# Weight halves for the output projection prepared by GpSimd one stage sooner, a third output tile begun early, and loads of the seam put behind dense products

## The chip, the cores and the metric

One core of one Trainium2 chip. The metric is the device time of one execution in microseconds; a smaller time is better. The engines are named as in the profile: PE is TensorE (matrix products; PEld its weight loads), DVE is VectorE, ACT is ScalarE, POOL is GpSimd, SP is SyncE, which here does nothing but issue DMA transfers.

## What is computed

One layer of a hybrid model over 2048 latent tokens and 128 context tokens, 1024 channels, all in float32. Cut to what matters:

```python
h = rmsnorm(x) * (1 + scale) + shift
proj = h @ w_in                                    # 1024 -> 4096
r, k, v, g_a, b_gate, c_gate, u_conv, g_b = split(proj)
r, k, v = token_shift(r, k, v)
# 8 heads of 64 channels, run forwards and backwards over the tokens:
#   S = S * w_t - (S kk_t) (kk_t a_t)^T + v_t k_t^T ;  y_t = S r_t
ya, s_final = wkv(h, r, k, v, s0)                  # group norm and bonus inside
ya = ya * silu(g_a)
yb = b_gate * short_conv(c_gate * u_conv) * silu(g_b)
u  = concat([ya, yb]) @ w_out                      # 1024 -> 1024
out = rmsnorm(x + gate * u)                        # and s_final of the context
```

The first 512 rows of `w_out` meet the recurrent half `ya` (called ATT in the kernel, k = 0 to 3 in blocks of 128), the last 512 the convolution half `yb` (CONV, k = 4 to 7). `yb` needs nothing of the recurrence.

## The kernel before, in words

Phase 1 is the input projection and the convolution half, in thirds of the tokens. Each of its products is kept near float32 by splitting both operands into a high part in the reduced format fp32r and the remainder: hi x hi, hi x lo, lo x hi, three matmuls for one. `yb` and, later, `ya` go to a scratch tensor `mixT` in memory.

Phase 2 is the recurrence in chunks of 64 tokens. It has 17 stages (`NST`), each of two groups of 8 chunk-and-head units, one for each direction; one of them is for the context. A stage is made of generators: `partL` loads its operands, `partI` solves its triangular systems (`solve_steps`, on POOL for most stages, `by_vector` on DVE for two), `partW` makes `psF`, `psG` and their results, `partB` makes `psX` and `psE`, `partU` makes `psU` and `psW` from `zc` (the loaded result of the solve, transposed to `zr`), and `partS` runs the state recurrence `psS` with `sv` and ends with `psT` and the group norm on `y`. The letters of the strings `ROUND` and, for the last two stages, `ROUND_END` give the order in which the generators of stage s (S, own B) and of stage s + 1 (L, u/U, B) are advanced. So while the states of stage s run, stage s + 1 is prepared. `early()` runs the first stage's parts inside the last dense products of phase 1; this place is called the seam (about 900 to 1005 us).

Phase 3 is the output projection: 17 tiles of 128 tokens, each of two halves of 512 columns, each half of 8 k-blocks of three matmuls of 128x512. `load_raw` loads a block of `w_out` (tile `woraw`), `load_k` makes its high part `woh` and its remainder `wol`; `load_m` does the same with 128 tokens of `mixT` (`mxc`, `mhc`, `mlc` for the convolution half, `mxa`, `mha`, `mla` for the recurrent one). The raw tiles `woraw`, `mxc` and `mxa` share two buffers of one tag, so a load waits until both readers of the tile before the last are done. Two output tiles, 5 and 6, have their convolution half done ahead, in the last stages of phase 2: the generator `ahead()` is advanced after each S of the ring. It first makes the four convolution weights, then for each tile the 12 products of each half into `psa`, stored in `z0`. `tail()` goes on with the recurrent weights and the full tiles (`psu`).

The written order is only the start. The queue of each engine is set by a scheduler that runs a simulated timeline over all the code, so an instruction may stand far ahead of its place in the text when its inputs and its tile are there. `behind(instruction, after)` adds an order between two instructions without a wait for data. On one engine the queue is then strictly in order; SP's queue holds nearly all loads and stores. `spare` puts a tile into the place of an operand that is no longer used.

## Time and profile before

| what | value |
|---|---|
| time, three runs | 1651.35, 1651.52, 1659.19 us, median 1651.52 |
| the profiled execution | 1657.8 us, span 1656.0 us |
| mean granted clock of TensorE | 0.969 |
| busy | PE 1538.7 us, DVE 1108.4, ACT 766.8, POOL 569.0 |
| transfers | 327.23 MB, mean 198 GB/s |
| phase 1 | to about 1005 us |
| the last POOL solve | stored at 1317.04 us |
| first product of phase 3 | 1466.21 us |

Times inside the profile count from the start of the span. The profiled execution lies 6.3 us above the median of the runs, as one of the three runs does. A busy row of the page divides the span into 40 slices of 41.4 us, a digit for each, in tenths.

### The profile page before, as it was taken

The numbers are of one execution on the slowest core, as the hardware profiler recorded it, in microseconds if no ns is written. First come the engines' busy times: TensorE is split into PE (matmuls) and PEld (weight loads), VectorE is DVE, ScalarE is ACT, GpSimd is POOL, SyncE is SP. The second block draws the span as 40 slices with busy tenths as digits, with TensorE's granted clock in tenths as the row PEclk, the third lists the DMA queues.
The fourth block names the chain that finished last, engine by engine and source line by source line (L and its number), as shares of the span: only waits on it lengthen the run. The fifth ranks groups of instructions, "written<-read, shape, count | busy, mean of one in ns | idle before, by whom it ended". The sixth has DMA issues, their size and how long they took to land.

```text
span 1656.0 us, 42386 instructions
## 1 busy us (share of the span) xinstructions
PE 1538.7 (93%) x17160; PEld 1412.4 (85%) x17160; DVE 1108.4 (67%) x2226; ACT 766.8 (46%) x1623; POOL 569.0 (34%) x1028
## 2 busy tenths in 40 slices
PE   5899999999999999999999899988988888789998
PEld 2899998999999999999988898878887777668886
DVE  5876977784738775658787883576775765574333
ACT  4544565553425353435554013667675665432222
POOL 0011211110102121112765564888888700022221
PEclk8899999999999999999999999999999989889999
DMA  9677767664746465655858768676767643264342
GB/s 377 205 263 249 244 234 276 218 225 178 241 140 208 166 207 183 200 202 186 271 165 270 237 201 239 179 192 180 204 175 195 169 131 102 66 198 160 127 149 93
DMA packets 237988, 327.23 MB, mean 198 GB/s; under 512 B 91288, under 2 KB 191896, under 8 KB 223712
## 3 DMA queue, kind: packets, MB, share of 16 engines
q1 hardware_dynamic: 231840, 318.55, 60.8%
q0 software_dynamic: 1200, 3.93, 0.6%
q8 instruction: 135, 2.21, 0.6%
q10 hardware_dynamic: 4752, 2.04, 0.5%
q14 instruction: 61, 0.50, 0.1%
HBM read 207.92 MB, written 116.54 MB: 196 GB/s over the span
## 4 chain that ended last, share of the span: by engine, by line
PE 47%; DVE 10%; ACT 7%; DMA 4%; issue 3%; POOL 3%; SPq 0%; DVEq 0%; ACTq 0%; POOLq 0%
PE psu L1380 4%; PE psu L1381 4%; PE psu L1382 4%; PE psE L840 3%; PE psS L840 2%; ACT fg L829 2%; PE psX L840 2%; PE psW L840 1%; PE mmg L166 1%; PE mmg L168 1%; PE mmg L167 1%; PE mmc L166 1%; PE mmc L167 1%; PE mmu L167 1%; PE mmu L166 1%
## 5 line engine op out<-in xcount | busy, mean ns | idle before, releaser
L950 POOL TENSOR_TENSOR zt<-zt,ztmp 128x30 f32<-128x30 f32 (+7 forms) x390 | 153.3, 393 | 30.6
L840 PE MATMUL psE<-fg 128*64 128x128 f32 x2176 | 135.8, 278 | 17.4 <-ACT fg L831 15.2
L840 PEld LDWEIGHTS psE<-fg 128*64 128x64 f32 x2176 | 120.8, 139 | 24.1 <-ACT fg L831 17.8
L840 PE MATMUL psS<-sv,E 128*64 128x64 f32 x2176 | 99.5, 235 | 19.3 <-DVE sv L1147 18.4
L840 PEld LDWEIGHTS psS<-sv,E 128*64 128x64 f32 x2176 | 82.5, 144 | 35.5 <-DVE sv L1147 24.4
L329 POOL TENSOR_TENSOR shk<-rawl 128x384 f32<-128x384 f32 (+1 forms) x24 | 24.8, 1033 | 242.9 <-ACT rawl L325 223.8
L829 ACT ACTIVATE fg<-psX 64x512 f32<-64x512 f32 x136 | 80.4, 591 | 44.9 <-PE psX L840 42.8
L1147 DVE TENSOR_TENSOR sv<-psS,pc 64x128 f32<-64x128 f32 x254 | 63.9, 277 | 43.6 <-PE psS L840 41.4
L947 POOL TENSOR_TENSOR ztmp<-ab,zt 128x60 f32<-128x60 f32 (+4 forms) x165 | 85.1, 516 | 12.9
L1447 POOL TENSOR_TENSOR z<-z,x 128x512 f32<-128x512 f32 x32 | 41.7, 1304 | 138.3 <-DVE z L1443 114.8
L329 POOL TENSOR_TENSOR shv<-rawl 128x384 f32<-128x384 f32 (+1 forms) x24 | 20.8, 866 | 164.5 <-ACT rawl L325 164.4
L1041 DVE TENSOR_TENSOR F<-psF,consts 128x512 f32<-128x512 f32 x68 | 44.0, 681 | 46.5 <-PE psF L840 46.5
L831 ACT COPY fg<-psG 64x256 f32<-64x256 f32 x136 | 49.8, 366 | 52.4 <-DVE fg L1048 46.3
L1048 DVE TENSOR_TENSOR fg<-psG,consts 64x256 f32<-64x256 f32 x136 | 57.3, 421 | 24.0 <-ACT fg L831 11.7
L166 PE MATMUL mmc<-h,w 128*128 128x384 f32 (+1 forms) x192 | 64.8, 337 | 5.9 <-ACT q1r L327 4.1
L446 POOL COPY pcs<-pp 128x6 f32<-128x6 f32 (+1 forms) x48 | 21.0, 437 | 139.2 <-ACT pp L435 138.9
L166 PE MATMUL mmg<-h,w 128*128 128x384 f32 (+1 forms) x192 | 64.3, 335 | 3.8 <-ACT q1v L327 3.8
L831 ACT COPY E<-psE 128x256 f32<-128x256 f32 x136 | 48.4, 373 | 37.8 <-DVE E L1109 27.9
L1109 DVE TENSOR_TENSOR E<-psE,consts 128x256 f32<-128x256 f32 x136 | 53.0, 418 | 19.0 <-PE psE L840 17.6
L166 PE MATMUL mmb<-h,w 128*128 128x384 f32 (+1 forms) x192 | 62.9, 328 | 1.5 <-ACT ta L439 1.5
L166 PE MATMUL mmgb<-h,w 128*128 128x384 f32 (+1 forms) x192 | 64.0, 333 | 0.3 <-ACT q1r L327 0.3
L168 PE MATMUL mmg<-h,w 128*128 128x384 f32 (+1 forms) x192 | 64.0, 334 | 0.0
(323 smaller groups left out, 5173.3 us busy)
## 6 DMA issues: line engine op xcount, KB each, us to landing
w<-scr_wsp SPq DMA_DIRECT2D x68, 1024.0 KB, 5.7
scr_wsp<-w SPq DMA_DIRECT2D x34, 1024.0 KB, 4.9
scr_ops<-pair SPq DMA_DIRECT2D x80, 384.0 KB, 4.0
wr<-in_win SPq DMA_DIRECT2D x34, 512.0 KB, 5.9
o<-scr_ops SPq DMA_DIRECT2D x32, 512.0 KB, 6.6
fg<-scr_ops SPq DMA_DIRECT2D x120, 128.0 KB, 3.5
x<-in_x SPq DMA_DIRECT2D x17, 512.0 KB, 8.5
wadas<-in_wada SPq DMA_DIRECT2D x8, 1024.0 KB, 13.5
```

The costliest lines, as they stand in the source:

```text
L166: T.matmul(ps[:, :n], w[:, 0, k], hh[:, 0, k, :n], start=k == 0, stop=False)
L168: K.dense = T.matmul(ps[:, :n], w[:, 1, k], hh[:, 0, k, :n], start=False, stop=k == 7).ins
L829: P.activation(dst, src, AF.Copy, scale=-1.0)
L831: P.copy(dst, src)
L840: r = T.matmul(*a, start=True, stop=True, **k)
L947: eng.tensor_tensor(tv, ab[:, j:j + 2, j + 2:32].unsqueeze(1).broadcast_to((128, kn, 2, n)), zt[:, :kn, j:j + 2].unsqueeze(3).broadcast_to ...
L950: last = eng.tensor_tensor(zt[:, :kn, j + 2:32], zt[:, :kn, j + 2:32], tv[:, :, r], ALU.subtract).ins
L1048: V.tensor_tensor(g.gs[H[1 - h], g.op, h, us], ps[gi][r, :, 64:128], B.mG[r, g.d].unsqueeze(1).broadcast_to((64, 4, 64)), ALU.mult)
L1147: r = V.tensor_tensor(dst, sp[gi][0:64, q], B.pc[0:64, d, 2 * p:2 * p + 2, c:c + 1].broadcast_to((64, 2, 64)), ALU.mult)
L1380: T.matmul(ps[:], mh[:, n], hi[:, cs], start=start and n == 0, stop=False)
L1381: T.matmul(ps[:], mh[:, n], lo[:, cs], start=False, stop=False)
L1382: T.matmul(ps[:], ml[:, n], hi[:, cs], start=False, stop=stop and n == 3)
```

## The change

It has two places. In the late stages: the four convolution weights and their halves are made by POOL (`G`) in place of ACT (`P`) and DVE (`V`); so are the halves of the tokens that go with them. `weights()` and `ahead()` start one stage sooner (s == NST - 4), and only the PSUM pool stays where it was (`open_sums`). The order of the weights is 6, 7, 4, 5, since 4 and 5 lie in places of operands that are in use longer. A third tile, 7, is done ahead, and `products` is called for one k-block, three matmuls, at a time. At the seam: the stores of the two solves on DVE are kept and issued behind dense products that come later, the loads of stage 1 are put behind such products too (`B.mid`), and `center_states` is cut in two.

```diff
+        store = lambda by: by(S["zt"][s].rearrange("h u s b q i -> (h u s b) (q i)"), zf)
+        if eng is G:
+            store(G.dma_start)
+        else:
+            B.kept.append([3, store])
...
-                load_half(g, half(g, n), D)
+                load_half(g, half(g, n), D if s != 1 else lambda *a: behind(D(*a), B.mid[1 if n else g.d]))
...
+    def put_back():
+        for x in B.kept:
+            x[0] -= 1
+        while B.kept and B.kept[0][0] <= 0:
+            behind(B.kept.pop(0)[1](D), K.dense)
+            B.mid.append(K.dense)
...
+            if s == NST - 4:
+                K.weights()
+                tail = K.ahead()
             if s == NST - 3:
                 O.pm.close()
                 O.pm = None
-                K.weights()
-                tail = K.ahead()
+                K.open_sums()
...
-    AHEAD = TILES[:2]
+    PREP = (6, 7, 4, 5)
+    AHEAD = TILES[:3]
...
+        copy = P.copy if raw is None else G.tensor_copy
         raw = raw or load_raw(k)
-        P.copy(hi[:], raw[:])
+        copy(hi[:], raw[:])
...
-        P.copy(mh[:], mx[:])
-        V.tensor_tensor(ml[:], mx[:], mh[:].bitcast(F32), ALU.subtract)
+        copy(mh[:], mx[:])
+        eng.tensor_tensor(ml[:], mx[:], mh[:].bitcast(F32), ALU.subtract)
...
-        for n, k in enumerate(CONV):
-            load_k(k, *[...], V, O.raw[n])
+        for n, k in enumerate(PREP):
+            load_k(k, *[...], G, O.raw[n])
             if n < 2:
-                O.raw.append(load_raw(CONV[n + 2]))
-            yield
+                O.raw.append(load_raw(PREP[n + 2]))
+            if n != 1:
+                yield
+            else:
+                for _ in range(5):
+                    yield
         for i in AHEAD:
-            ms = load_m(O.r, i, CONV, 1)
+            ms = load_m(O.r, i, CONV, 1, G.tensor_copy, G)
...
-                products(ps, ms, HALF[h], CONV, True, True)
+                for n in range(4):
+                    products(ps, ms, HALF[h], CONV, True, True, n)
+                    if n < 3:
+                        yield
                 P.copy(z0[i][:, HALF[h]], ps[:])
                 yield
```

What the scheduler makes of it shows in the queues. First POOL, from the store of the last solve (`scr_zt`) to the recurrent weights; `sv` is the tile of the states that is set to zero for a stage, `held` its value kept for the next. Before:

```order
L955 DMA scr_zt_66<-zt_1124_15938 128x512
L970 MEMSET sv_1207_17780 64x128 x4
L970 MEMSET sv_1208_17786 64x128 x4
L1129 COPY sv_1231_18310<-held_1219_18159 64x128
L1129 COPY sv_1232_18312<-held_1220_18166 64x128
L1361 TENSOR_TENSOR wol1_18861<-woraw1_18862,woh1_18860 128x1024
L1361 TENSOR_TENSOR wol0_18855<-woraw0_18856,woh0_18854 128x1024
L1361 TENSOR_TENSOR wol2_18867<-woraw2_18868,woh2_18866 128x1024
L1361 TENSOR_TENSOR wol3_18873<-woraw3_18874,woh3_18872 128x1024
```

After:

```order
L955 DMA scr_zt_66<-zt_1124_15938 128x512
L1385 CAST woh4_17675<-woraw4_17448 128x1024
L1386 TENSOR_TENSOR wol4_17676<-woraw4_17448,woh4_17675 128x1024
L1397 CAST mhc5_17913<-mxc5_17911 128x512
L1398 TENSOR_TENSOR mlc5_17914<-mxc5_17911,mhc5_17913 128x512
L974 MEMSET sv_1207_17796 64x128 x4
L974 MEMSET sv_1208_17802 64x128 x4
L1385 CAST woh5_17871<-woraw5_17486 128x1024
L1386 TENSOR_TENSOR wol5_17872<-woraw5_17486,woh5_17871 128x1024
L1397 CAST mhc6_18394<-mxc6_18392 128x512
L1398 TENSOR_TENSOR mlc6_18395<-mxc6_18392,mhc6_18394 128x512
L1397 CAST mhc7_18813<-mxc7_18811 128x512
```

`woh4` to `mlc6` stand behind the last solve, the casts and subtracts of tile 5 ahead of the two memsets, those of `woh5` and tile 6 behind them; tile 7's and the four recurrent `wol` follow.

The other two weights, 6 and 7, stand much earlier on POOL, inside a solve (`ztmp` and `zt` are its tiles; the row numbers are from 357 on of 791):

```order
L947 TENSOR_TENSOR ztmp_911_11021<-ab_909_11015,zt_910_11020 128x220
L950 TENSOR_TENSOR zt_910_11020<-zt_910_11020,ztmp_911_11021 128x5x22
L1385 CAST woh6_17444<-woraw6_17300 128x1024
L950 TENSOR_TENSOR zt_910_11020<-zt_910_11020,ztmp_911_11021 128x5x22
L1385 CAST woh7_17482<-woraw7_17302 128x1024
L1386 TENSOR_TENSOR wol6_17445<-woraw6_17300,woh6_17444 128x1024
L947 TENSOR_TENSOR ztmp_911_11021<-ab_909_11015,zt_910_11020 128x240
L1386 TENSOR_TENSOR wol7_17483<-woraw7_17302,woh7_17482 128x1024
L950 TENSOR_TENSOR zt_910_11020<-zt_910_11020,ztmp_911_11021 128x6x20 x2
L947 TENSOR_TENSOR ztmp_911_11021<-ab_909_11015,zt_910_11020 128x252
```

Before, the same place holds the solve's rows alone.

SP at that time, early in phase 2 (`woraw` are the raw weights, `zc` the solve's result for stage 2, `ab` the next solve's input). Before:

```order
L1185 DMA sg_965_12528<-scr_sg_61 128x512
L1354 DMA woraw4_17735<-in_wout 128x1024
L1354 DMA woraw5_17737<-in_wout 128x1024
L998 DMA fg0_9816<-scr_ops0_57 64x2x256 x2
L998 DMA fg1_9817<-scr_ops1_58 64x2x256 x2
L889 DMA a1_10972<-scr_lo_65 128x256 x2
L1027 DMA zc_933_11608<-scr_zt_66 64x16x32 x2
L925 DMA ab2_913_11102<-scr_at_64 32x1024 x4
L987 DMA sv_931_11604<-scr_vt_60 64x1024
L987 DMA sv_932_11606<-scr_vt_60 64x1024
```

After:

```order
L1190 DMA sg_965_12528<-scr_sg_61 128x512
L1378 DMA woraw6_17300<-in_wout 128x1024
L1378 DMA woraw7_17302<-in_wout 128x1024
L1003 DMA fg0_9816<-scr_ops0_57 64x2x256 x2
L1003 DMA fg1_9817<-scr_ops1_58 64x2x256 x2
L889 DMA a1_10972<-scr_lo_65 128x256 x2
L1378 DMA woraw4_17448<-in_wout 128x1024
L1378 DMA woraw5_17486<-in_wout 128x1024
L1032 DMA zc_933_11608<-scr_zt_66 64x16x32 x2
L992 DMA sv_931_11604<-scr_vt_60 64x1024
L992 DMA sv_932_11606<-scr_vt_60 64x1024
```

All four raw weights now go out here; 4 and 5 take the buffers of 6 and 7, whose readers are on POOL.

SP in the late stages, with the token blocks `mxc` and the operands of the stage that comes next. Before:

```order
L1354 DMA woraw6_17895<-in_wout 128x1024
L1001 DMA fg0_9816<-scr_ops0_57 64x2x128 x4
L1001 DMA fg1_9817<-scr_ops1_58 64x2x128 x4
L1354 DMA woraw7_17933<-in_wout 128x1024
L1369 DMA mxc5_18058<-scr_mixT_63 128x4x128
L1001 DMA fg0_9816<-scr_ops0_57 64x2x128 x4
L1001 DMA fg1_9817<-scr_ops1_58 64x2x128 x4
L1369 DMA mxc6_18169<-scr_mixT_63 128x4x128
L1185 DMA sg_1203_17739<-scr_sg_61 128x512
L1027 DMA zc_1209_17792<-scr_zt_66 64x16x32
L1221 DMA scr_mixT_63<-yo_1198_17535 128x512
L1027 DMA zc_1209_17792<-scr_zt_66 64x16x32
```

After:

```order
L1006 DMA fg0_9816<-scr_ops0_57 64x2x128 x4
L1006 DMA fg1_9817<-scr_ops1_58 64x2x128 x4
L1394 DMA mxc5_17911<-scr_mixT_63 128x4x128
L1394 DMA mxc6_18392<-scr_mixT_63 128x4x128
L1006 DMA fg0_9816<-scr_ops0_57 64x2x128 x4
L1006 DMA fg1_9817<-scr_ops1_58 64x2x128 x4
L1190 DMA sg_1203_17755<-scr_sg_61 128x512
L1032 DMA zc_1209_17808<-scr_zt_66 64x16x32
L1226 DMA scr_mixT_63<-yo_1198_17554 128x512
L1032 DMA zc_1209_17808<-scr_zt_66 64x16x32
```

The two raw weights are gone from here, and tile 6's `mxc6` stands ahead of the second four-piece loads `fg`.

PE, where the products of tile 7 (`psa7`) are put, between the group norm's `psT` and `psW`, `psF` and `psX` of stage 15. Before:

```order
L840 MATMUL psS14_0_4_17986<-sv_1187_17334,E_1213_17857 64x64 x4
L840 MATMUL psS14_1_4_17992<-sv_1188_17336,E_1214_17869 64x64 x4
L847 MATMUL psT1215_18002<-consts_9809,y_1091_15179 128x2x64 x4
L840 MATMUL psW15_18011<-zc_1209_17792,zr_1212_17855 32x32 x32
L840 MATMUL psS14_0_4_17986<-sv_1187_17334,E_1213_17857 64x64 x4
L840 MATMUL psS14_1_4_17992<-sv_1188_17336,E_1214_17869 64x64 x4
L840 MATMUL psF15_0_1_18087<-fg0_9816,o30_10973 64x128 x2
L840 MATMUL psF15_1_1_18088<-fg1_9817,o31_10974 64x128 x2
```

After:

```order
L840 MATMUL psS14_0_4_18007<-sv_1187_17341,E_1213_17877 64x64 x4
L840 MATMUL psS14_1_4_18013<-sv_1188_17343,E_1214_17889 64x64 x4
L847 MATMUL psT1215_18023<-consts_9809,y_1091_15179 128x2x64 x4
L1407 MATMUL psa7_0_18818<-woh4_17675,mhc7_18813 128x512
L1408 MATMUL psa7_0_18818<-wol4_17676,mhc7_18813 128x512
L1407 MATMUL psa7_1_18832<-woh4_17675,mhc7_18813 128x512
L1408 MATMUL psa7_1_18832<-wol4_17676,mhc7_18813 128x512
L840 MATMUL psW15_18032<-zc_1209_17808,zr_1212_17875 32x32 x32
L840 MATMUL psS14_0_4_18007<-sv_1187_17341,E_1213_17877 64x64 x4
L840 MATMUL psS14_1_4_18013<-sv_1188_17343,E_1214_17889 64x64 x4
L840 MATMUL psF15_0_1_18091<-fg0_9816,o30_10973 64x128 x2
```

Four of tile 7's 24 products stand here; sixteen more follow behind the first `psX15`, four in `psG15`. Up to this place PE's order is the same in both kernels but for the places of `psa5` and `psa6`.

More of the change, by code (lines that the diff above doesn't have):

```diff
@@ L954, in solve_steps @@
             O.solved = last
-        (G.dma_start if eng is G else D)(S["zt"][s].rearrange("h u s b q i -> (h u s b) (q i)"), zf)
+        store = lambda by: by(S["zt"][s].rearrange("h u s b q i -> (h u s b) (q i)"), zf)
[3 more added lines that the diff above has]
+            B.kept.append([3, store])
     def by_vector(s, d):
@@ L1226, in phase2 @@
     K.mixed = {}
+    def put_back():
[4 more added lines that the diff above has]
+            B.mid.append(K.dense)
     def early():
         setup_first()
-        center_states()
+        B.kept, B.mid = [], []
+        center = center_states()
+        next(center)
         partI(2)
@@ L1236, in early @@
         sts[0] = partL(0, K.dense)
+        for _ in center:
+            pass
         next(vec)
@@ L1243, in early @@
             next(vec, None)
+            put_back()
             yield
@@ L1248, in early @@
             next(vec, None)
+            put_back()
             yield
@@ L1251, in early @@
             pass
+        while B.kept:
+            put_back()
         B.bb = bb
@@ L1357, in load_k, with load_m @@
     def load_k(k, hi, lo, eng, raw=None):
+        copy = P.copy if raw is None else G.tensor_copy
         raw = raw or load_raw(k)
-        P.copy(hi[:], raw[:])
+        copy(hi[:], raw[:])
         eng.tensor_tensor(lo[:], raw[:], hi[:].bitcast(F32), ALU.subtract)
         wk[k] = (hi, lo)
-    def load_m(pool, i, ks, b):
+    def load_m(pool, i, ks, b, copy=P.copy, eng=V):
         t0 = i * 128
@@ L1371, in load_m, with products @@
         ml = pool.tile([128, 4, 128], F32R, tag=f"ml{a}", name=f"ml{a}{i}", bufs=b)
-        P.copy(mh[:], mx[:])
-        V.tensor_tensor(ml[:], mx[:], mh[:].bitcast(F32), ALU.subtract)
+        copy(mh[:], mx[:])
+        eng.tensor_tensor(ml[:], mx[:], mh[:].bitcast(F32), ALU.subtract)
         return mh, ml
-    def products(ps, ms, cs, ks, start, stop):
+    def products(ps, ms, cs, ks, start, stop, only=None):
         mh, ml = ms
         for n, k in enumerate(ks):
+            if only not in (None, n):
+                continue
             hi, lo = wk[k]
@@ L1387, in weights, with open_sums @@
         O.r = Pool(K, "p3r", "left")
+        O.raw = [load_raw(k) for k in PREP[:2]]
+    def open_sums():
         O.pr = Pool(K, "p3pr", "right", 2, PSUM)
         O.pu = O.pr
-        O.raw = [load_raw(k) for k in CONV[:2]]
     def ahead():
         yield
-        for n, k in enumerate(CONV):
-            load_k(k, *[K.spare(f"wo{a}{k}", F32R, f"o{k - 3}{m}") if n < 2 else O.r.tile([128, 1024], F32R, name=f"wo{a}{k}") for m, a in enumerate("hl")], V, O.raw[n])
+        for n, k in enumerate(PREP):
+            load_k(k, *[K.spare(f"wo{a}{k}", F32R, f"o{k - 3}{m}") if k < 6 else O.r.tile([128, 1024], F32R, name=f"wo{a}{k}") for m, a in enumerate("hl")], G, O.raw[n])
             if n < 2:
-                O.raw.append(load_raw(CONV[n + 2]))
-            yield
+                O.raw.append(load_raw(PREP[n + 2]))
[4 more added lines that the diff above has]
+                    yield
         for i in AHEAD:
-            ms = load_m(O.r, i, CONV, 1)
+            ms = load_m(O.r, i, CONV, 1, G.tensor_copy, G)
             if i not in z0:
-                z0[i] = K.spare(f"z0_{i}", F32, "ab2" if z0 else "ab")
+                z0[i] = K.spare(f"z0_{i}", F32, ("ab", "ab2")[len(z0)]) if len(z0) < 2 else O.r.tile([128, 1024], F32, name=f"z0_{i}")
             for h in range(2):
                 ps = O.pr.tile([128, 512], F32, tag="u", name=f"psa{i}_{h}")
-                products(ps, ms, HALF[h], CONV, True, True)
+                for n in range(4):
+                    products(ps, ms, HALF[h], CONV, True, True, n)
+                    if n < 3:
+                        yield
                 P.copy(z0[i][:, HALF[h]], ps[:])
@@ L1463, in rest @@
             p.close()
-    K.weights, K.ahead, K.tail, K.rest = weights, ahead, tail, rest
+    K.weights, K.open_sums, K.ahead, K.tail, K.rest = weights, open_sums, ahead, tail, rest
 def layout3(I):
```

## The prediction

> **What bounds the kernel now.** I read the page first, then the late part in windows cut at the first matmul of each stage's `psU`, then what TensorE waits for in each window, then the groups of the operations that change hands.

> ```profile
> PE 1538.7 (93%) x17160; PEld 1412.4 (85%) x17160; DVE 1108.4 (67%) x2226; ACT 766.8 (46%) x1623; POOL 569.0 (34%) x1028
> PE   5899999999999999999999899988988888789998
> PE 47%; DVE 10%; ACT 7%; DMA 4%; issue 3%; POOL 3%; SPq 0%; DVEq 0%; ACTq 0%; POOLq 0%
> ```

> TensorE is busy 93% of the span and holds 47% of the chain that ended last, so time is won only where its row shows less than 9, or by taking matmuls off it. The change takes none off it. Its row has one long weak stretch, the 8s and the 7 from the 27th digit on (each digit is 41.4 us). The windows show that stretch stage by stage; I call them window 13 (from psU13 to psU14, the third row), 14, 15 and 16, and the last row is the start of phase 3.

> ```profile
> core 0: us, PE busy (x) PEld busy (x) DVE busy (x) ACT busy (x) POOL busy (x), PEclk, DMA share, GB/s
> 1194.10:1218.70 24.60, 21.96 (x586) 19.56 (x586) 18.49 (x45) 15.04 (x32) 21.23 (x48) 1.00 0.72 193
> 1298.90:1322.10 23.20, 21.47 (x588) 19.42 (x588) 18.40 (x45) 15.00 (x32) 15.95 (x34) 1.00 0.69 187
> 1322.10:1353.90 31.80, 25.20 (x582) 21.77 (x583) 20.10 (x47) 20.65 (x40) 0.00 (x0) 0.89 0.47 126
> 1353.90:1394.30 40.40, 38.05 (x632) 31.64 (x630) 18.05 (x45) 21.11 (x42) 1.26 (x8) 0.87 0.37 102
> 1394.30:1423.20 28.90, 23.91 (x570) 20.74 (x570) 18.77 (x45) 15.62 (x33) 2.91 (x3) 0.94 0.32 84
> 1423.20:1466.20 43.00, 28.72 (x604) 24.39 (x604) 27.44 (x69) 19.14 (x37) 7.43 (x3) 0.86 0.45 142
> 1466.20:1512.00 45.80, 45.79 (x192) 37.06 (x193) 27.03 (x41) 13.47 (x33) 11.95 (x9) 0.95 0.54 173
> ```

> An undisturbed stage lasts 23.2 to 24.6 us. Window 13 has the same count of matmuls (582) and lasts 31.8: ACT is up from 15.0 to 20.65 us, DVE from 18.4 to 20.1, POOL does nothing. Window 14 holds 48 more products. Phase 3 runs TensorE without a gap, 192 products in 45.79 us, 0.2385 us each. What TensorE waits for, window by window (13; 14; 15; 16 with the first product of phase 3):

> ```profile
> PE psS L840 <- DVE sv L1147: 2.6, 2, 1.6
> PE psF L840 <- ACT E L831: 2.0, 1, 2.0
> PE psE L840 <- ACT fg L831: 1.1, 1, 1.1
> PE psG L840 <- ACT fg L829: 0.5, 1, 0.5
> ...
> PE psE L840 <- ACT fg L831: 2.0, 1, 2.0
> ...
> PE psE L840 <- ACT fg L831: 3.3, 1, 3.3
> PE psF L840 <- ACT fg L829: 1.1, 1, 1.1
> ...
> PE psT L847 <- DVE y L1202: 4.4, 1, 4.4
> PE psu L1380 <- ACT mha L1372: 4.1, 1, 4.1
> ```

> **The change, part by part.** First what it takes from ACT and DVE in windows 13 and 14. The rows are the cast of a weight block on ACT, its subtract on DVE, the same subtract where GpSimd does it already, and the largest one-input operation that GpSimd has (a memset of half that width):

> ```profile
> L1360 ACT CAST woh<-woraw x4: 1034/1044/1044, 1333.1 to 1367.2; 128x1024 fp32r<-128x1024 f32 x4
> L1361 DVE TENSOR_TENSOR wol<-woraw,woh x4: 1173/1225/1226, 1334.2 to 1368.3; 128x1024 fp32r<-128x1024 f32 x4
> L1361 POOL TENSOR_TENSOR wol<-woraw,woh x4: 2336/2346/2778, 1406.5 to 1456.5; 128x1024 fp32r<-128x1024 f32 x4
> L935 POOL MEMSET zt<- x13: 524/529/533, 900.7 to 1289.0; 128x512 f32 x13
> 1317.04 0.61 POOL L955 DMA_DIRECT2D scr_zt<-zt  x1 [0.30 <-POOL zt L950]
> 1364.13 0.63 POOL L970 MEMSET sv<- 64x128 f32 x4 [46.48 <-PE psS L840]
> ```

> Three of the four casts and subtracts (1333 to 1348 us) fall into window 13: 3 x 1.04 = 3.1 us of ACT and 3 x 1.22 = 3.7 us of DVE, between a chain PE to ACT to DVE to PE that waits for these two engines by turns (6.2 us of waits in the rows above). With them on GpSimd, which ends its last solve at 1317.04 and then idles 46.48 us, window 13 has the work of the row 1194.1 or 1298.9. I take 24.5, the worse of them: **-7.3 us** (-8.6 at 23.2; 0 if the stall only moves). Nobody waits for GpSimd there as long as its copies end in time. A cast on GpSimd has no row: from below two memset widths, 1.06 us, from above the two-input subtract, 2.35 us; I take 1.1, since it has one input like the memset. Two weight blocks and tile 5's halves are then 2 x (1.1 + 2.35) + 0.55 + 1.2 = 8.7 us of GpSimd time, or 11.9 at the upper price, in some 45 free ones.

> Window 14 first pays for the gaps of window 13 with a lower clock:

> ```profile
> 1336.00:1343.00 7.00, 4.40 (x84) 3.11 (x84) 4.08 (x8) 3.81 (x9) 0.00 (x0) 0.88 0.63 164
> 1343.00:1362.00 19.00, 17.17 (x356) 15.66 (x357) 10.64 (x26) 11.39 (x23) 0.00 (x0) 0.68 0.37 111
> 1362.00:1374.00 12.00, 9.65 (x197) 8.23 (x198) 7.16 (x17) 7.95 (x18) 1.26 (x8) 0.92 0.61 164
> ```

> After 2.6 us of gaps in 1336 to 1343 the granted clock is 0.68 until 1362. Of that, 8.1 us lie in window 14: 8.1 x 0.32 = 2.6 us, and 12 x 0.08 = 1.0 after it; not all of a stage goes by the clock, so I take 2.8 of the 3.6. With the 2.0 us of waits in this window, 40.4 would become 35.6; its floor is 23.5 + 48 x 0.2385 = 34.9. No single wait in these windows before it was longer than 2.0 us. [...] I add 0.4 for what is late next: tile 6's halves now wait on GpSimd behind the two `sv` memsets (1364.13 above, which the shorter window 13 moves to about 1357), `woh5`, `wol5`, `mhc6`, `mlc6`, in all 1.4 + 1.1 + 2.35 + 3 us for its load + 1.75, so about 1367, and its products come 24 products after tile 5's, which begin at 1373.7 - 7.3 = 1366.4. So **-4.4 us** (-5.5 at the floor, 0 with the clock and the waits as they are).

> Window 15 takes tile 7's 24 products, 24 x 0.2385 = 5.7 us, in pieces after `psT`, inside `psX15` and inside `psG15`. If they fill the 4.4 us of waits, it lasts 28.9 - 4.4 + 5.7 = 30.2; if the chain is pushed back whole, 34.6. Pieces of three products (0.7 us) can stand in a wait of 3.3, but 16 of them stand in one row ahead of `psX15`, which the next wait hangs on. I take 32.0: **+3.1** (+1.3 to +5.7). Window 16: nothing changes in its order on the chain, which goes from the last weight blocks of GpSimd through `mha` to `psu` (4.1 us above): **0**. Phase 3 has 24 products less and no gap to swallow them: -5.7, of which I give 0.4 back for tile 7's store and adds: **-5.3**.

> What the earlier start costs: the pool of the weights is now there at once, and the program puts the first two loads and their cast and subtract into the middle of a solve at about 1025 us. On SP the third and fourth load then wait for GpSimd to be done with the first two, and `zc`, `ab` and `sv` queue behind them.

> ```profile
> 1021.56 1.22 SPq L1354 DMA_DIRECT2D woraw<-in_wout  x2
> 1027.58 2.88 SPq L1027 DMA_DIRECT2D zc<-scr_zt  x2
> woraw<-in_wout SPq DMA_DIRECT2D x2, 512.0 KB, 5.9
> 1042.64 0.69 DVE L1055 STREAM_TRANSPOSE zr<-zc 128x512 f32<-128x512 f32 x1
> ```

> The loads land at 1021.6 + 5.9 = 1027.5; two casts and two subtracts (6.9 us) end at 1034.4; `zc` goes out at about 1035 in place of 1027.6, which leaves 7.6 us to its transpose at 1042.64, about what a load of that size takes here (5.9). The solves all come some 9 us later, but the last ended at 1317 for a stage that loads its result after 1390. I take **+2.0** (0 if `zc` lands in time; +8 if all 7.4 us of the delay reach TensorE; nearer to 0 by the 7.6 us).

> At the seam TensorE has two waits between 900 and 1008 us:

> ```profile
> PE psG L840 <- DVE F L1041: 3.9, 1, 3.9
> PE psF L840 <- DVE fg L950: 1.3, 1, 1.3
> ```

> Both are on DVE, whose order and TensorE's are the same in both kernels there; only SP's issues move. **-0.2** (-5.2 if both go, +1 if a load comes late).

> Sum: -7.3 - 4.4 + 3.1 + 0 - 5.3 + 2.0 - 0.2 = -12.1 us. The profiled execution took 1657.8 us (span 1656.0), so 1645.7 in its terms; the runs shown are 1651.35, 1651.52 and 1659.19, and against their median the same sum gives 1639.4, which I round to **1639.5**. 0.5% is 8.3 us, about what a measurement can tell from no change: under 1643.3 is faster, over 1659.8 slower.

> **The rivals.**
> Better than the sum: `zc` lands in time, window 13 comes to 23.4, window 15 takes the products in its waits: -12.1 - 2.0 - 1.1 - 1.8 = -17, 1634.5. For it speak the 7.6 us and the 4.4 us of waits; against it, that an edit at so many places seldom goes without a new wait.
> The stall of window 13 stays: its waits are a dependence chain (`psF` on `E`, `psS` on `sv`) and the copies only stood beside it. Then -7.3 falls away: -4.8, 1646.7. Against it: windows with the same chain and no copies last 23.2 to 24.6.
> The third tile pays nothing: window 15 is pushed back by all 5.7: -9.5, 1642; with a like push of window 14 (2.7) by late halves of tile 6, -6.8, 1644.7.
> [...]
> GpSimd against DVE: with the copies beside them, DVE's operations get longer. The rows are of DVE's `y` subtract with GpSimd solving (1075 to 1317 us) and with GpSimd mostly idle (1317 to 1466):

> ```profile
> L1202 DVE TENSOR_TENSOR y<-y,yss 128x512 f32<-128x512 f32 x10 | 7.8, 785 | 0.1
> L1202 DVE TENSOR_TENSOR y<-y,yss 128x512 f32<-128x512 f32 x6 | 4.1, 689 | 0.2
> ```

> 14% longer beside a busy GpSimd, 1.2 us on 8.7 us of copies; if instead DVE stood still for each of them, 8.7 us come back less the DVE work removed (4.9 in all four subtracts), some 4, and with the lateness behind it up to 8: 1643 to 1648. [...]
> Slower: SP is one queue in order, and it now holds loads that wait for GpSimd. In window 14 the load of tile 6's halves waits for `wol5`, which stands behind the `sv` memsets; behind it stand the stage's second `fg` loads, `sg` and `zc` of stage 15.

> ```profile
> 1350.17 5.95 SPq L1001 DMA_DIRECT2D fg<-scr_ops  x8
> 1359.05 0.61 SPq L1027 DMA_DIRECT2D zc<-scr_zt  x1
> 1384.38 0.69 DVE L1055 STREAM_TRANSPOSE zr<-zc 128x512 f32<-128x512 f32 x1
> ```

> Before, `zc` went out at 1359.05 and was used at 1384.38, 25 us later; with `wol5` done at 1361 and 8 us of issues behind it, it goes out at about 1368 against a use at about 1377, 9 us later. A GpSimd copy that takes twice the upper price uses this up, and then each us late is a us of TensorE, there and at 1035. The gain of 12 is gone, and 8.3 lost, once 20 us are late in the two places: 1660 and over.

> **How the numbers follow.** The sum as forecast, -8 to -16: 0.46. Better: 0.14. The stall stays: 0.12. The third tile pays nothing: 0.10. The low clock stays: 0.04. GpSimd against DVE: 0.06. The held queue, slower: 0.08. Faster by over 0.5% are the first two but for 0.03 at the edge, and 0.03 each of the third tile's case and the clock's: 0.63. Slower 0.08, the rest 0.29. The forecast's own range is 1635.5 to 1643.5. The range to hold 8 in 10 reaches down to 1630, below the better case, and up to 1651, over the stall that stays and GpSimd against DVE; it leaves out the slower case and a few in a hundred at each end.

> **What would show it.** After: window 13 near 24.5 with its casts gone from ACT and DVE and POOL at some 8 us; the clock near 1.00 at its end; window 14 near 36; `psa` in three tiles, 72 products, the last 24 in a window 15 near 32; 24 `psu` products fewer. At 1021 to 1045, whether `zr` waits for `zc`. I am wrong if window 13 stays above 28, if a GpSimd cast takes over 2.4 us, if SP shows loads waiting for GpSimd with TensorE's wait on `fg` or `zr` behind them, or if the two waits of the seam go.

## The result, and the profile after

| | before | changed |
|---|---|---|
| median of 20 runs each (lowest to highest) | 1655.89 us (1650.55 to 1661.42) | 1648.16 us (1643.41 to 1654.59) |
| ratio (95% interval) | | 0.9958 (0.9947 to 0.9969) |
| the profiled execution's span | 1656.0 us | 1652.1 us |

The change gains 7.7 us by the medians, 0.42% by the ratio. The time lies in the stated range (1630 to 1651), but the sum was -12.1, and windows 13 and 14, which were meant to pay most, paid more than forecast, so something else took the difference. (The forecast 1639.5 counted from a median of three runs, 1651.52; the twenty give 1655.89, so 4.4 of the 8.7 us between 1639.5 and 1648.16 are that starting point.) The late windows of the changed kernel, 12 to 16, cut at the first matmul of `psU` as before (the columns are those shown before):

```profile
1309.94:1333.04 23.10, 21.43 (x585) 19.38 (x581) 18.30 (x45) 15.01 (x32) 16.98 (x37) 1.00 0.68 185
1333.04:1356.31 23.27, 21.31 (x585) 19.30 (x581) 16.16 (x43) 17.34 (x36) 4.71 (x4) 1.00 0.45 120
1356.31:1391.04 34.73, 33.52 (x632) 28.04 (x629) 16.17 (x43) 19.70 (x40) 7.76 (x14) 1.00 0.44 116
1391.04:1424.29 33.25, 29.76 (x593) 24.79 (x589) 18.56 (x45) 16.68 (x35) 4.57 (x4) 0.95 0.33 89
1424.29:1467.56 43.27, 28.92 (x609) 24.58 (x605) 27.63 (x69) 19.16 (x37) 7.44 (x3) 0.85 0.45 144
```

Window 13 is an undisturbed stage now (31.8 to 23.3 us), window 14 goes from 40.4 to 34.7 at a clock of 1.00, window 15 from 28.9 to 33.3, window 16 stays. What TensorE waits for in windows 13, 14 and 15 of the changed kernel:

```profile
PE psS L840 <- DVE sv L1152: 1.7, 2, 1.4
PE psG L840 <- ACT fg L829: 0.2, 1, 0.2
...
PE psS L840 <- DVE sv L1152: 1.2, 2, 0.9
...
PE psE L840 <- ACT E L831: 2.2, 1, 2.2
PE psF L840 <- ACT fg L829: 1.0, 1, 1.0
```

Against that, windows 7 to 11, in which the change alters nothing, take longer. The whole stretch of windows 7 to 11, first of before, then of the changed kernel:

```profile
1170.60:1298.85 128.25, 113.10 (x2905) 101.14 (x2901) 88.61 (x221) 79.25 (x168) 110.70 (x247) 0.96 0.69 184
...
1172.42:1309.94 137.52, 118.31 (x2904) 105.70 (x2901) 89.23 (x221) 79.35 (x168) 118.77 (x263) 0.91 0.67 174
```

The same instructions, 9.3 us more, at a lower clock (0.91 against 0.96). TensorE's waits in this stretch, before and then changed:

```profile
PE psF L840 <- issue: 3.0, 2, 2.5
PE psW L840 <- issue: 2.3, 1, 2.3
PE psE L840 <- issue: 0.9, 1, 0.9
...
PE psW L840 <- issue: 7.3, 3, 3.1
PE psF L840 <- issue: 5.1, 2, 2.7
```

"issue" is a wait that no semaphore of the profile ends: TensorE stops in the middle of a run of like matmuls. These stops are 12.4 us in the changed kernel and 6.2 us before. The matmuls between them take 118.3 us in place of 113.1, and the other waits come to some 2 us less. Here is one, by time, in window 8 of the changed kernel:

```profile
1199.03 1.20 PE L840 MATMUL psU<-zr,a 32*32 32x32 f32 x64
...
1201.36 1.22 PE L840 MATMUL psW<-zc,zr 32*32 32x32 f32 x57
1205.14 0.31 PE L840 MATMUL psW<-zc,zr 32*32 32x32 f32 x7 [2.57 <-issue]
```

57 of 64 `psW` products, 2.57 us of nothing, then the other 7. GpSimd's solves had moved as well. These are the two weights that the change brings into the solve at 1025 us, and when they ran:

```profile
1029.06 1.03 POOL L1385 CAST woh<-woraw 128x1024 fp32r<-128x1024 f32 x1 [3.31 <-DMA woraw<-in_wout]
...
1031.48 1.04 POOL L1385 CAST woh<-woraw 128x1024 fp32r<-128x1024 f32 x1 [1.00 <-DMA woraw<-in_wout]
1032.48 2.36 POOL L1386 TENSOR_TENSOR wol<-woraw,woh 128x1024 fp32r<-128x1024 f32 x1
...
1035.36 2.35 POOL L1386 TENSOR_TENSOR wol<-woraw,woh 128x1024 fp32r<-128x1024 f32 x1
```

6.8 us of work and 4.3 us of waits: the solve ends some 11 us later, and so does every solve after it, since they run back to back (GpSimd waits for nothing from 1036 to 1320 us). The `zt` store, which ends a solve, came at 3.6, 7.3, 12.5, 15.5 and 19.7 us into windows 6 to 10 before, at 14.1, 18.4, 19.5, 21.0 and 21.0 now.

### The profile page after: what moved, and what is told of

Its sections match the earlier page's. It is cut to its first block, busy times and chain, and to the rows that moved or that the text cites. A ratio compares the mean times of both kernels' runs of the same rounds, so it can differ in the third digit from the quotient of the medians.

```text
span 1652.1 us, 42387 instructions
## 1 busy us (share of the span) xinstructions
PE 1535.0 (93%) x17160; PEld 1408.0 (85%) x17160; DVE 1104.5 (67%) x2221; ACT 764.3 (46%) x1618; POOL 592.0 (36%) x1042
## 3 DMA queue, kind: packets, MB, share of 16 engines
q8 instruction: 135, 2.21, 0.6%
## 4 chain that ended last, share of the span: by engine, by line
PE 48%; DVE 11%; ACT 6%; DMA 4%; issue 4%; POOL 1%; SPq 0%; DVEq 0%; ACTq 0%; POOLq 0%
PE psE L840 4%; PE psu L1407 3%; PE psu L1408 3%; PE psu L1409 3%; PE psS L840 3%; PE psX L840 2%; ACT fg L829 2%; PE psF L840 1%; PE psW L840 1%; DVE E L1114 1%; PE psG L840 1%; PE mmc L166 1%; PE psU L840 1%; PE mmc L167 1%; PE mmu L167 1%
## 5 line engine op out<-in xcount | busy, mean ns | idle before, releaser
L950 POOL TENSOR_TENSOR zt<-zt,ztmp 128x30 f32<-128x30 f32 (+7 forms) x390 | 156.2, 401 | 30.4
L840 PE MATMUL psE<-fg 128*64 128x128 f32 x2176 | 135.4, 279 | 12.4 <-ACT fg L831 9.8
L840 PEld LDWEIGHTS psE<-fg 128*64 128x64 f32 x2176 | 121.1, 140 | 18.7 <-ACT fg L831 11.9
L840 PE MATMUL psS<-sv,E 128*64 128x64 f32 x2176 | 99.2, 234 | 19.0 <-DVE sv L1152 17.8
L840 PEld LDWEIGHTS psS<-sv,E 128*64 128x64 f32 x2176 | 82.1, 144 | 35.2 <-DVE sv L1152 22.6
L829 ACT ACTIVATE fg<-psX 64x512 f32<-64x512 f32 x136 | 80.5, 592 | 44.7 <-PE psX L840 42.6
L329 POOL TENSOR_TENSOR shv<-rawl 128x384 f32<-128x384 f32 (+1 forms) x24 | 20.8, 867 | 166.6 <-ACT rawl L325 166.5
L1053 DVE TENSOR_TENSOR fg<-psG,consts 64x256 f32<-64x256 f32 x136 | 57.4, 422 | 25.5 <-ACT fg L831 13.8
L831 ACT COPY fg<-psG 64x256 f32<-64x256 f32 x136 | 49.9, 367 | 45.5 <-DVE fg L1053 39.4
L166 PE MATMUL mmc<-h,w 128*128 128x384 f32 (+1 forms) x192 | 64.8, 338 | 5.9 <-ACT q1r L327 4.1
L166 PE MATMUL mmg<-h,w 128*128 128x384 f32 (+1 forms) x192 | 64.0, 334 | 3.8 <-ACT q1v L327 3.8
L831 ACT COPY E<-psE 128x256 f32<-128x256 f32 x136 | 48.5, 373 | 36.2 <-DVE E L1114 26.8
L167 PE MATMUL mmc<-h,w 128*128 128x384 f32 (+1 forms) x192 | 64.2, 334 | 0.0
## 6 DMA issues: line engine op xcount, KB each, us to landing
wr<-in_win SPq DMA_DIRECT2D x34, 512.0 KB, 6.2
o<-scr_ops SPq DMA_DIRECT2D x32, 512.0 KB, 6.6
x<-in_x SPq DMA_DIRECT2D x17, 512.0 KB, 3.8
```

Source lines behind the costliest of these rows:

```text
L166: T.matmul(ps[:, :n], w[:, 0, k], hh[:, 0, k, :n], start=k == 0, stop=False)
L167: T.matmul(ps[:, :n], w[:, 0, k], hh[:, 1, k, :n], start=False, stop=False)
L829: P.activation(dst, src, AF.Copy, scale=-1.0)
L831: P.copy(dst, src)
L840: r = T.matmul(*a, start=True, stop=True, **k)
L950: last = eng.tensor_tensor(zt[:, :kn, j + 2:32], zt[:, :kn, j + 2:32], tv[:, :, r], ALU.subtract).ins
```

## The experiments

Each kernel ran on one chip together with the kernel before, and ratios are against those runs. Kernels that ran at different times or on different chips are compared by their ratios, and "us" of such a comparison are worked out from these. The theories named in the expectations are A (the solves that come later against the stages), B (only the queue at 1030 us) and C (chance of a run).

**e1, the hoist undone.** The loads of the first two weights get an order behind the last matmul written before the stage in which the weights begin (`K.first`).

```diff
-        O.raw = [load_raw(k) for k in PREP[:2]]
+        O.raw = [load_raw(k, K.first) for k in PREP[:2]]   # behind(load, K.first)
```

> The changed kernel with one thing undone: the first two weight loads are ordered behind the last matmul written before the stage in which the weights pool is opened, so that neither they nor their casts and subtracts stand at 1025 us in the middle of a solve; they come after the last solve. Theory A (late solves): at 1025 us GpSimd lost some 11 us, all later solves came 9 to 11 us later against the stages, the load of the next solve's input then fell ahead of the stage's psU and psW, and TensorE stood there for its instructions (issue) in windows 7, 8 and 9 besides 10 and 11; without the hoist these three windows return to 23.5 to 24.6 us and the gain over the kernel before grows from 7.7 us to 15 to 18 us (ratio 0.989 to 0.991). Theory B (the queue alone): only the 2 us that windows 1 to 2 lost come back, ratio 0.994 to 0.995, and windows 7 to 9 stay at 26 to 28. Theory C (chance of a run): windows 7 to 9 differ from run to run whatever the order; ratio near 0.995 with no pattern.

Measured: 1641.05 us, ratio 0.9910 (0.9883 to 0.9937), some 15 us below before by the ratio. Windows 7 to 9 go back to 24.0, 24.5 and 23.5 us, and windows 7 to 11 together to 129.8 from 137.5, so B is out. For C there is this much: the four profiles without a delay and with the solves' loads in their old place (before, e1, e3, e7) have 127.7 to 132.3 us in windows 7 to 11, and e7 has 26.2 and 25.6 in windows 8 and 9. But e7 fits A: its stages reached psU7 at 1164.3 in place of 1170.6 before, while its solve ended at 1178.6 in place of 1177.9, so that its solves, too, were late against the stages. Not all of the 10.6 us that the changed kernel lost between psU1 and psU13 shows in the time, because window 14 took 39.3 in place of 34.7: the last weight copies were late there.

```profile
1166.30:1296.10 129.80, 113.42 (x2906) 101.29 (x2902) 89.39 (x221) 79.28 (x168) 111.99 (x249) 0.95 0.68 182
...
PE psa L1410 <- POOL wol L1388: 1.0, 1, 1.0
PE psS L840 <- issue: 0.9, 1, 0.9
PE psa L1409 <- POOL woh L1387: 0.8, 1, 0.8
```

**e2, the delay alone.** The kernel before with 18 memsets more on GpSimd in that solve (10.4 us in the trace), and nothing else.

```diff
+            if eng is G and s == 6 and m == 5:
+                for _ in range(18):
+                    eng.memset(tmp[:], 0.0)
```

> The kernel before with 18 memsets of 0.53 us each added on GpSimd in the middle of the solve that runs at 1025 us (a tile that is written anew after it), 9.5 us, and nothing else. Nothing waits for these memsets but the later solves. Theory A: windows 7, 8 and 9 go to 26 to 28 us with issue waits of TensorE at psW or psF, and the kernel is 7 to 11 us slower than before (ratio 1.004 to 1.007). Theory B: no change beyond 1 us, since the last solve ends at 1317 for a result that is loaded after 1390. Theory C: no change.

Measured: 1664.05 us, ratio 1.0052 (1.0032 to 1.0072), 8.6 us slower by the ratio (5.3 to 11.9). Here 10.4 us of work that no instruction of TensorE waits for, on an engine off the path with over 70 us to spare at its end (1317 to 1390), cost 8.6 us. The time came as theory A said, the windows did not. Windows 7, 8 and 9 took 24.8 to 25.4 us, not 26 to 28, and window 10 took 31.0. Windows 7 to 11 together took 134.4, 6 more than before, and only 4.7 us of them are "issue". In windows 8 to 10 `o` and `fg`, the operands of the next stage, went out at or behind psU itself (`o` at 1246.55 for a psU10 at 1243.85), and in window 10 TensorE waited for `fg` (1.1 us) and for what ACT makes of it (4.4 us). So the late loads cost time here in part as late operands. Another 2.8 us stand in window 14, at a clock of 0.80 against 0.87.

**e3, the seam alone.** The kept stores, the loads behind `B.mid` and the split of `center_states`, on the kernel before.

> The seam's part of the change alone, on the kernel before: the kept stores of the two solves on VectorE, the loads of stage 1 behind dense products, the split of the centering. The prediction said -0.2 us. The changed kernel's trace has 4.4 us of waits at the seam where before had 5.2, and stage 1's psU 0.5 us later. Expected by that reading: within 1.5 us of before (ratio 0.999 to 1.001). A rival: the loads that go later fall on other transfers and the stage after pays for it, 2 to 4 us slower (1.001 to 1.0025).

Measured: 1655.47 us, ratio 1.0001 (0.9978 to 1.0024). The seam's part is worth nothing that can be measured.

**e5, e10, e11: the solves' input loads in another place.** A solve takes its input from `ab`, of which there are two; SP's load of the next one but one waits until the running solve has read its last (8.2 us in window 8 of the changed kernel). The edit moves the load of the later solves' input from the end of a stage to behind the next stage's group norm, and orders it behind a matmul there (from stage 13's solve on in e5 and e10, `LATE = 13`; from stage 12's in e11, `LATE = 12`).

```diff
-            if 1 <= s and s + 7 < NST:
+            if 1 <= s and s + 7 < NST and s + 7 < LATE:
                 partI(s + 7)
...
                 elif c == "T":
                     for f in todo:
                         run(f)
+                    if LATE <= s + 6 < NST:
+                        partI(s + 6, K.first)
```

e5 is this on e1:

> The kernel of e1 with one more edit: the input loads of the last four solves (ab of stages 13 to 16) are written behind the group norm of the next stage, in place of the end of a stage. Theory A with the load as the cause: the two waits for instructions that the kernel before has in windows 10 and 11 (2.3 and 2.5 us, windows of 26.4 and 30.3 us) go too, and it is 4 to 8 us faster than e1 (ratio to before 0.985 to 0.988). Rival: it is not the load but the solve's store, or the sum of all loads, that holds the instructions up; then windows 10 and 11 stay as they are, ratio as e1. A second rival: the solves wait for their later inputs, the last result comes too late, and the kernel is slower than e1.

Measured: 1639.18 us, ratio 0.9892 (0.9860 to 0.9924), 3 us below e1 and within the interval; the 4 to 8 us of the expectation did not show. Windows 7 to 11 took 121.9 us at a clock of 1.00, 8 less than in e1, as A said. In this profile windows 1 to 6 took 6.2 us more than in e1 (155.0 against 148.8), at a clock of 0.91 against 0.97. The queues of the two kernels are the same up to there, so this is a difference between executions and not of the edit.

e10 is this on the kernel before:

> The kernel before with one edit: the input loads of the last four solves behind the next stage's group norm, nothing else. If these loads, falling just ahead of psU and psW, hold TensorE's instructions up, windows 10 and 11 (26.4 and 30.3 us before) go to 24 to 26 and the kernel gains 6 to 9 us (ratio 0.9945 to 0.9965). Rival: the solve's own end, its store, is what collides; windows 10 and 11 stay and the ratio is 1.000.

Measured: 1648.84 us, ratio 0.9970 (0.9951 to 0.9988), 5 us faster, just under the 6 to 9 expected. Windows 10 and 11 took 24.7 and 25.3 us, and windows 7 to 11 together 122.2, against 128.3 before. So the kernel before paid this too, in windows 10 and 11.

e11 is this on the changed kernel, hoist and late solves left in:

> The changed kernel, hoist and late solves and all, with the input loads of the last five solves behind the next stage's group norm. The solves still end 9 to 11 us later than before against the stages. If the loads' place is the cause, windows 8 to 11 come back to 23.5 to 25.5 us although the solves are late, and 9 to 12 us are won on the changed kernel (ratio to before 0.988 to 0.991). Rival: the lateness of the solves itself (their store beside psU) is the cause; windows 8 to 11 stay at 26 to 30 and the ratio stays at 0.995 to 0.997.

Measured: 1637.95 us, ratio 0.9892 (0.9873 to 0.9911), and once more, beside e12 to e14, 1634.60 us, 0.9871 (0.9844 to 0.9898); these second runs are named e11b. It is the fastest kernel of the study, by the ratios 18 to 21 us below before and 11 to 14 below the changed one. Windows 7 to 11 of e11b:

```profile
1172.30:1195.60 23.30, 21.40 (x584) 19.34 (x580) 18.83 (x47) 14.81 (x32) 20.21 (x44) 1.00 0.75 208
1195.60:1219.50 23.90, 21.62 (x584) 19.45 (x580) 18.45 (x45) 15.01 (x32) 20.65 (x47) 1.00 0.72 200
1219.50:1242.80 23.30, 21.33 (x585) 19.30 (x582) 16.25 (x43) 17.34 (x36) 19.93 (x44) 1.00 0.74 196
1242.80:1266.30 23.50, 21.55 (x583) 19.44 (x580) 16.57 (x43) 17.34 (x36) 20.45 (x44) 1.00 0.73 203
1266.30:1290.80 24.50, 21.78 (x587) 19.56 (x583) 19.16 (x47) 14.86 (x32) 21.13 (x48) 1.00 0.78 199
```

All undisturbed, at full clock, with solves that end about as late as in the changed kernel (12.0, 16.4 and 20.8 us into windows 6 to 8, and the next two only after their window). It is thus not the late solve that costs but the place of its load. SP's queue by time shows what the place does, first in the changed kernel, then in e11b, for the same loads at the end of window 8 (window 9 begins, with its psU, at 1225.1 and at 1219.5):

```profile
1208.14 1.45 SPq L1190 DMA_DIRECT2D w<-scr_q  x1
1217.51 2.56 SPq L925 DMA_DIRECT2D ab<-scr_at  x4
1220.17 1.12 SPq L992 DMA_DIRECT2D sv<-scr_vt  x2
1221.38 1.05 SPq L882 DMA_DIRECT2D o<-scr_ops  x2
1222.53 9.53 SPq L1003 DMA_DIRECT2D fg<-scr_ops  x8
...
1206.57 1.27 SPq L883 DMA_DIRECT2D o<-scr_ops  x2
1209.14 10.83 SPq L1004 DMA_DIRECT2D fg<-scr_ops  x8
...
1220.69 1.77 SPq L926 DMA_DIRECT2D ab<-scr_at  x4
```

In the changed kernel SP issues nothing from 1209.6 to 1217.5: `ab` stands at the head and waits for GpSimd (8.2 us for `zt`, by SP's own waits). Behind it stand the next stage's `o` (two of 512 KB) and `fg` (eight of 128 KB), which go out from 1221.4 to 1232, across the 64 `psU` and 64 `psW` products at 1225 to 1229. In e11b the same `o` goes out 13 us ahead of psU and the last `fg` as psU begins, and `ab` follows behind them with a wait of 0.4 us. The first 8 us of windows 8, 9 and 10 in the changed kernel and in e11b:

```profile
1199.00:1207.00 8.00, 5.43 (x184) 4.85 (x184) 4.35 (x10) 2.57 (x5) 6.90 (x15) 0.92 0.95 231
1225.10:1233.10 8.00, 5.43 (x199) 4.64 (x195) 4.87 (x12) 4.43 (x8) 6.94 (x14) 0.99 0.91 235
1252.80:1260.80 8.00, 4.92 (x178) 4.41 (x180) 2.85 (x8) 3.30 (x6) 6.90 (x15) 0.97 0.81 192
...
1195.60:1203.60 8.00, 7.18 (x248) 6.16 (x244) 5.99 (x14) 3.44 (x7) 6.83 (x16) 1.00 0.79 227
1219.50:1227.50 8.00, 7.09 (x248) 6.09 (x244) 5.28 (x13) 5.21 (x10) 6.90 (x15) 1.00 0.81 229
1242.80:1250.80 8.00, 7.15 (x247) 6.15 (x244) 5.42 (x13) 4.97 (x9) 7.10 (x17) 1.00 0.65 201
```

Some 248 matmuls and as many weight loads in 8 us when it goes well, 178 to 199 in these three windows of the changed kernel. How busy the DMA engines are does not separate the two (0.81 stands on both sides, and window 7 of the changed kernel made only 202 matmuls at 0.65). The place of `o` does so better: over windows 7 to 11 of all fourteen profiles, 17 of the 20 windows in which `o` goes out within 6 us of psU have a stop of more than 1 us in their first 10 us, and 3 of the other 50.

What TensorE waits for can be read from the packets that the traces hold. The page counts 135 transfers of instructions on their largest queue (q8) with 2.21 MB, 16.4 KB each. TensorE has 34,659 instruction records in the changed kernel's trace, so one transfer for some 257. Between 1010 and 1310 us the fourteen traces have 45 "issue" stops of more than 0.8 us. If these records are counted in blocks of 256, all 45 end at the same place of a block, give or take one record, and all end 1.2 to 1.7 us after such a transfer has ended. In the five of windows 7 to 11 of the changed kernel, that transfer began 3.0 to 4.0 us after TensorE had passed the same place of the block before; at the same five places of e11b it began after 0.8 to 1.7 us, and TensorE stopped for at most 0.6. So I read a stop as a wait for the next block of instructions, whose transfer comes late where `o` and `fg` go out beside it. No run took the instruction transfers themselves away; this reading rests on their times and on what the place of `o` and `fg` changes.

**e7, ACT and DVE in place of GpSimd**, on e1: start one stage sooner, three tiles and pieces kept.

```diff
-        copy = P.copy if raw is None else G.tensor_copy
+        copy = P.copy
...
-            load_k(k, *[...], G, O.raw[n])
+            load_k(k, *[...], V, O.raw[n])
...
-            ms = load_m(O.r, i, CONV, 1, G.tensor_copy, G)
+            ms = load_m(O.r, i, CONV, 1)
```

> The kernel of e1 (no hoist) with the convolution weights' and halves' copies on ScalarE and their subtracts on VectorE, as in the kernel before; the start one stage sooner, the third tile and the pieces stay. If it is GpSimd that frees window 13 (the prediction's reading), window 13 goes from 23.3 in e1 back to 28 to 32 us and the kernel is 5 to 8 us slower than e1 (ratio to before 0.994 to 0.996). Rival: it is the earlier start and not the engine; window 13 stays below 25 and the time is that of e1 (0.990 to 0.992).

Measured: 1651.27 us, ratio 0.9976 (0.9957 to 0.9995), some 11 us slower than e1 by the ratios, more than the 5 to 8 expected; its profile also has 2.5 us more in windows 7 to 11. Window 13 takes 30.9 us with ACT back at 20.90 us and DVE at 20.34:

```profile
1320.70:1351.60 30.90, 23.98 (x586) 21.31 (x582) 20.34 (x47) 20.90 (x41) 0.00 (x0) 0.93 0.61 171
PE psS L840 <- DVE sv L1152: 3.5, 2, 2.5
PE psG L840 <- ACT fg L829: 2.3, 1, 2.3
```

It is the engine that frees window 13 (23.3 us in e1), not the earlier start.

**e9, e14: the first two weight loads at two other places, with the solves' loads moved.** e9 is e5 with them behind a matmul one stage ahead of e1's (`LATE = 13`); e14 is e11 with them behind a matmul of stage 6 (`LATE = 12`).

> The kernel of e5 (no hoist, the last four solves' inputs behind the next stage's group norm) with the first two weight loads one stage sooner than there, behind a matmul of the stage before. In e1 and e5 the copies of the last weight blocks were late in window 14 (39.3 and 36.9 us, waits on woh and wol); here they should be ready as in the changed kernel, whose window 14 took 34.7. Expected 2 to 5 us below e5: 1634 to 1638, ratio to before 0.987 to 0.989. Rival: the loads now fall into window 12 with the stage's own and TensorE waits there for instructions; same as e5.

Measured: 1640.24 us, ratio 0.9904 (0.9886 to 0.9922): no better than e5. Window 14 came to 34.7 as expected and windows 7 to 11 stood at 23.2 to 24.7, but window 13 took 29.7, with 4.9 us of wait of `psE` on `fg`. Window 12, which the rival named, took 23.8.

> The kernel of e11 with the first two weight loads ordered behind a matmul of stage 6, so that their casts and subtracts stand between two solves at about 1150 us and not inside one at 1025, and SP is not held at 1030. If the 3.5 us that windows 1 and 2 show against before (29.5 and 26.4 in e11, 27.9 and 24.0 before) are the held queue, 2 to 4 us below e11: ratio to before 0.986 to 0.989. Rival: the hold is only moved and its stage pays the same; as e11.

Measured: 1645.19 us, ratio 0.9939 (0.9917 to 0.9961), some 11 us slower than e11b: the hold is moved, as the rival said, and its stage pays far more. Windows 1 and 2 came to 49.9 us, from 54.1 in e11b; window 7 took 35.0. SP there:

```profile
1160.07 0.63 SPq L1004 DMA_DIRECT2D fg<-scr_ops  x1
1160.74 21.93 SPq L1383 DMA_DIRECT2D woraw<-in_wout  x2
1182.77 2.57 SPq L1004 DMA_DIRECT2D fg<-scr_ops  x4
```

The third weight load waits for GpSimd to have copied the first, GpSimd first ends its solve at 1177, and SP stands for some 22 us with the stage's `fg` behind it; `psE` then waits 8.9 us in one piece on ACT's `fg`. This is the mechanism of the prediction's slower rival.

**e12, two tiles**, and **e13, whole halves**, both on e11.

```diff
-    AHEAD = TILES[:3]
+    AHEAD = TILES[:2]
```

> The kernel of e11 with two output tiles done ahead in place of three. The changed kernel's trace had window 15 4.3 us longer than before and phase 3 5.3 us shorter, so the third tile is worth about 1 us: window 15 near 28.9, phase 3 5.3 us longer, 0 to 2 us slower than e11. Rival: what fills window 15 is free, as the prediction's better case had it, and the kernel is 4 to 6 us slower than e11.

Measured: 1640.83 us, ratio 0.9904 (0.9874 to 0.9934), against e11b's 1634.60: slower by some 6 us by the medians, with intervals that overlap, and so nearer to the rival than to the 0 to 2 us expected. By the two profiles the third tile saves 4.5 us in phase 3 (189.0 to 184.5) and costs 1.5 in window 15, which takes 31.8 us without its 24 products and 33.3 with them. One wait there shrinks from 5.8 us to 2.2 (e12, then e11b):

```profile
PE psE L841 <- ACT fg L832: 5.8, 1, 5.8
...
PE psE L841 <- ACT E L832: 2.2, 1, 2.2
```

> The kernel of e11 with each half's twelve products in one piece in place of four pieces of three. Theory: the pieces hardly matter, since the queue puts 16 of tile 7's products in one row anyway: within 1.5 us of e11, windows 14 and 15 within 1 us. Rival: pieces fill waits, and without them window 15 is 2 to 3 us longer.

Measured: 1636.77 us, ratio 0.9891 (0.9860 to 0.9923), 2 us from e11b, with intervals that overlap; windows 14 and 15 took 34.8 and 32.1 us. The pieces of three bring nothing that shows.

## Why the prediction was right or wrong

By its own terms, from the two profiled executions (before to changed):

| term | forecast | measured |
|---|---|---|
| window 13 | -7.3 | 31.87 to 23.27: -8.6 |
| window 14 | -4.4 | 40.40 to 34.73: -5.7 |
| window 15 | +3.1 | 28.86 to 33.25: +4.4 |
| window 16 | 0 | +0.2 |
| phase 3 | -5.3 | 189.79 to 184.54: -5.25 |
| the early hoist | +2.0 | psU1 to psU13 302.41 to 312.98: +10.6 |
| the seam | -0.2 | psU1 at 1019.59, now 1020.06: +0.5 |
| sum | -12.1 | -3.9 in these two executions, -7.7 by the medians |

**The step that failed** is the sentence on the hoist: "The solves all come some 9 us later, but the last ended at 1317 for a stage that loads its result after 1390." The slack was real and the price of zero was wrong. The step looked at who needs the solves' results; what mattered was who stands behind the solves' inputs. SP's `ab` load waits for GpSimd at the head of an in-order queue (8.2 us in window 8, with nothing issued from 1209.6 to 1217.5). Coming some 11 us later, it moves the next stage's 2 MB (two of 512 KB, eight of 128 KB) onto `psU` and `psW`. Of the +10.6, windows 7 to 11 have 9.3. e2 shows that such a delay alone costs time (+8.6, in part by operands that come late), e1 takes the 9.3 back but for 1.6, and e11 removes it with the solves as late as they were. The prediction's own rows leap from window 8 to window 12; windows 10 and 11 of the kernel before, 26.4 and 30.3 us with two "issue" stops, already showed the price.

The +2.0 itself, for `zc` and SP's hold at 1035, was too small by half. Windows 1 and 2 took 51.9 us before and 53.3 after in the two profiles, but single profiles scatter by 5 us: the nine without the hoist have 48.2 to 53.0, mean 50.3, and the five with it 51.5 to 56.1, mean 54.2, so about +4. The prediction let the two casts and subtracts end at 1034.4; they ended at 1037.7.

The better part of the forecast was right, the prices of its copies above all: a GpSimd cast takes 1.03 us (1.1 was taken), the subtract 2.36. Window 13 became the undisturbed stage that the copies had broken, and e7 shows that it was their engine. The low clock of window 14 went with the gaps, from 0.87 to 1.00, as the sum had it; the case that it stays, with its 0.04, did not come. That DVE stands still for GpSimd's copies, a term of the prediction's 1643 to 1648, no run shows: its 43 operations of window 13 take 16.16 us with 4.7 us of GpSimd work beside them, e1's, with 6.6 us, 16.18, and those of window 9 before, with 20.3 us of solving, 16.18. Phase 3 came out as forecast, and the seam's term was as small as it was set.

**Window 15** was forecast at +3.1 and measured at +4.4. Over all profiles the tile costs about what was forecast: with tile 7 the window takes 31.6 us in four profiles and 32.1 to 33.3 in the others, without it 28.8 to 29.2 in three. The 1.6 us between the changed kernel's 33.3 and 31.6 go with its clock, 0.95 against 1.00. e12 alone would mislead here: it has 31.8 us without tile 7, as e3 has 31.5, and in both DVE stood idle ahead of the transpose of the solve's result. DVE's queue in e12:

```profile
1386.55 0.71 DVE L1061 STREAM_TRANSPOSE zr<-zc 128x512 f32<-128x512 f32 x1 [2.34 <-issue]
...
1389.16 1.78 DVE L1054 TENSOR_TENSOR fg<-psG,consts 64x256 f32<-64x256 f32 x4
```

The transpose of the last stage's `zc`, which SP had sent for at 1378 to 1380, idles DVE for 2.3 us (1.6 in e3, at most 0.2 in the other twelve), and the `fg` that `psE` waits for stands behind it. That it is the load that ends this idle time is read from the order, not shown by a releaser, and whether leaving out tile 7 makes `zc` late is not shown. So the rival "the third tile pays nothing" was wrong: the tile costs some 3 us in window 15 and saves 5 in phase 3. The better case, which let the waits take the products for 1.3 us, is not shown either.

The slower rival named the right mechanism, a queue in order that holds loads which wait for GpSimd, and the wrong place: it looked for weight loads in window 14, where `psE`'s wait went away, and at 1035, where the hold cost about 4 us, and not at the `ab` load that had waited there all along.

## What to carry to other kernels

When work is added to an engine that is off the path, follow not only its results but its inputs: the load that refills its buffer waits for it at the head of a queue (here `ab`, 8.2 us), and what stands behind that load belongs to others (here the next stage's `o` and `fg`). A load that waits long for its buffer should stand behind the loads that do not wait; moving four or five such loads gained 5 us on the kernel before and 11 to 14 on the changed one. Windows that the change does not touch are to be compared first, with their waits "issue" and their clock: they showed in one row what no term of the sum had. One profile of a window is not enough where profiles of like kernels scatter by 5 us: windows 1 and 2, and window 15, read otherwise over all of them.
